# Issuing an activation exchange of 12 transfers a few at a time between weight loads, and placing the splits of an exchanged block ahead of the next transposition

## The chip, the cores and the metric

The kernel runs on one core of one Trainium2 chip. The metric is the device time of one execution in microseconds (us). Of the kernel before there are three timed runs, 964.92, 965.22 and 965.23 us; their median is 965.22 us.

## What is computed

A small encoder: two layers, 256 tokens of width 1024, all in 32-bit floats. Each layer has a feed-forward sub-layer, a token mixer (retention in the first layer, latent attention in the second) beside a cross-attention into 256 memory tokens, and a second feed-forward sub-layer. What the change touches is the feed-forward, of which there are four with inner width 2816:

```python
def swiglu(h, w_gu, w_down):
    g, u = jnp.split(h @ w_gu, 2, axis=-1)
    return (jax.nn.silu(g) * u) @ w_down

for l in range(DEPTH):
    x = x + 0.5 * rms_norm(swiglu(rms_norm(x, ng[0]), ffn_w_gu[l, 0], ffn_w_down[l, 0]), ng[1])
    ...
    x = x + 0.5 * rms_norm(swiglu(rms_norm(x, ng[4]), ffn_w_gu[l, 1], ffn_w_down[l, 1]), ng[5])
```

All weights are read from HBM once per execution, some 180 MB in all.

## The kernel before

**Matmuls.** The 256 tokens are two halves of 128, t = 0 and 1. A float32 product is made of three matmuls (`mm3`, L136 to L138) of operands that are split into a high part of reduced precision and a remainder: high times high, high times low, low times high. A split (`split`, L75 and L76) is a copy on ACT that makes the high part and a subtraction on DVE that makes the low one.

**Weights.** Weights go through tiles of 128 x 1024 floats, 512 KB each. `load_raw` (L79) fills a tile `raw` from HBM, there are five of them; a gate-and-up tile (four per chunk) takes two DMAs of 256 KB (L87), a down tile (two per chunk) one of 512 KB (L89). `split_raw` makes `wh` (ACT) and `wl` (DVE) of it, there are nine of each. So a tile can be loaded at most 14 tiles before the one that TensorE (PE) is working on. All these DMAs are issued by the SP queue, which works in order: a DMA whose semaphores have not come holds back those behind it.

**The feed-forward** (`ffn`) cuts the inner width into 11 chunks c of 256 columns. `gu(t, c)` makes gate and up of a chunk (24 matmuls), `swiglu(t, c)` makes `s` (ACT, L263) and `a` (DVE, L265). `both(c)` multiplies a chunk by its rows of the down weights for both halves (24 matmuls) and needs the chunk's activations with the inner width on the partitions. The order on PE is written out: (0,0), (0,1), (1,0), (1,1) in some order, then (0,2), (1,2), and from c = 3 on gu(0,c), gu(1,c), both(c-3).

**The exchange.** The turning of a chunk is done without PE. `turn(t, c)` (L277 ff.) has DVE transpose blocks of 32 x 32 (STREAM_TRANSPOSE, L282) into a tile `aT` that holds two chunks and both halves. After (1, c) with c odd, 16 pieces of 32 partitions x 256 floats have to change partitions, from `aT` to a tile `ag`, of which there is one: four stay on their partitions and are copied by POOL (L288), twelve are DMAs of 32 KB on the SP queue (L291). This happens at c = 1, 3, 5, 7 and 9 of each of four feed-forwards, 20 times. `take(c)` then splits a chunk of `ag` into `ah` and `al` for both halves, at the `swiglu` named by `landed`: chunk 0 at (0,3), chunk 1 at (1,3), chunk 2 at (0,5) and so on.

```python
if t == 1 and c % 2:
    g = wk.tile([P, 1024], F32, name="ag", tag="ag", bufs=1)
    for i in range(4):
        sl = slice(i * 32, (i + 1) * 32)
        G.tensor_copy(out=g[sl, i * 256:(i + 1) * 256], in_=b[sl, i * 256:(i + 1) * 256])
        for q in range(4):
            if q != i:
                nc.sync.dma_start(out=g[q * 32:(q + 1) * 32, i * 256:(i + 1) * 256],
                                  in_=b[sl, q * 256:(q + 1) * 256])
    pair[c - 1], pair[c] = g, g
```

**What sets the order.** PE's order is that of the program text. On ACT, DVE, POOL and SP a scheduler places instructions by its own estimate of when they are ready; `tc.issue_after(x)` (in `behind` and `behind_weights`) makes it place something behind x.

Of the kernel before, what the change touches and what calls it, by code (L numbers as in the profile page):

```python
# [31 lines left out]
def kernel(ctx, tc, x, mem, positions, norm_gains, ffn_w_gu, ffn_w_down, w_o,  # L32
                        mem_norm, mem_w_kv, ret_w_in, ret_log_decay, ret_head_norm,
                        mla_w_in, mla_q_norm, mla_kv_norm, mla_w_uq, mla_w_ukv, inv_freq, out):
    nc = tc.nc
    V, S, G, T = nc.vector, nc.scalar, nc.gpsimd, nc.tensor
# [17 lines left out]
    def k1(name, n=256, dt=F32):  # L54
        return wk.tile([P, n], dt, name=name, tag="k1", bufs=13)
# [4 lines left out]
    def bank():  # L60
        return ps.tile([P, 512], F32, name="bank", tag="bank")

    def raw_tile():
        return wp.tile([P, 1024], F32, name="raw", tag="raw", bufs=5)
# [12 lines left out]
        return ins  # L77

    def load_raw(src, cols):  # L79
        raw = raw_tile()  # L80
        dst = raw[:, :cols]
        if len(src.shape) == 3:
            dst = dst.rearrange("p (k n) -> p k n", k=src.shape[1])
        if len(src.shape) == 4:
            dst = dst.rearrange("p (k h n) -> p k h n", k=src.shape[1], h=src.shape[2])
            for k in range(src.shape[1]):
                last_load[0] = nc.sync.dma_start(out=dst[:, k], in_=src[:, k]).ins  # L87
        else:
            last_load[0] = nc.sync.dma_start(out=dst, in_=src).ins  # L89
        return raw  # L90

    last_load = [None]

    def behind_weights():

        return tc.issue_after(last_load[0])
# [3 lines left out]
    def behind(*inss):  # L100

        st = ExitStack()
        for i in inss:
            st.enter_context(tc.issue_after(i))
        return st
# [16 lines left out]
    def weights(src, cols):  # L122
        return split_raw(load_raw(src, cols), cols)
# [11 lines left out]
    def mm3(dst, ah, al, bh, bl, start, stop):  # L135
        T.matmul(out=dst, lhsT=ah, rhs=bh, start=start, stop=False)  # L136
        T.matmul(out=dst, lhsT=ah, rhs=bl, start=False, stop=False)  # L137
        T.matmul(out=dst, lhsT=al, rhs=bh, start=False, stop=stop)  # L138
# [65 lines left out]
    def post(t, accs, gain, half, next_gain, hook=None):  # L204
# [19 lines left out]
                hook()  # L224
        return None if next_gain is None else pre(t, next_gain)


    def gu_src(wgu, c, u):
        return (wgu[2 * u * P:(2 * u + 2) * P, :]
                .rearrange("(k p) (h f) -> p k h f", p=P, h=2)[:, :, :, c * FC:(c + 1) * FC])  # L230

    def ffn(l, j, zs, gains, extra=(), first=None):
        wgu, wd = ffn_w_gu[l, j], ffn_w_down[l, j]
        gu_w, d_w, act, at, pair = {}, {}, {}, {}, {}
        accs = [[None, None], [None, None]]
        extra = dict(extra)
        C = NFC - 1

        def load_gu(c):
            gu_w[c] = [weights(gu_src(wgu, c, u), 1024) for u in range(KB // 2)]  # L240

        def load_d(c):
            d_w[c] = [weights(wd[c * FC + b * P:c * FC + (b + 1) * P, :], 1024) for b in range(2)]

        def gu(t, c, part=None):
            z = zs[t]
            if c not in gu_w:
                load_gu(c)
            if part != 1:
                act[t, c] = bank()  # L250
            p = act[t, c]
            for k in range(KB) if part is None else range(part * 4, part * 4 + 4):
                wh, wl = gu_w[c][k // 2]
                n = slice((k % 2) * 512, (k % 2 + 1) * 512)
                m = slice(k * P, (k + 1) * P)
                mm3(p, z.h[:, m], z.l[:, m], wh[:, n], wl[:, n], k == 0, k == KB - 1)
            if part is None:
                swiglu(t, c)

        def swiglu(t, c):  # L260
            p, z = act[t, c], zs[t]
            s = k1("s")
            s_ins = S.activation(out=s, in_=p[:, 0:FC], func=AF.Silu, scale=z.r).ins  # L263
            a = k1("a")
            a_ins = V.scalar_tensor_tensor(out=a, in0=p[:, FC:2 * FC], scalar=z.r, in1=s,  # L265
                                           op0=ALU.mult, op1=ALU.mult).ins
            if (t, c) == (1, NFC - 1) or first and (t, c) == (0, 0):
                ahead[:] = [s_ins, a_ins]
            act[t, c] = a
            if c < C:  # L270
                turn(t, c)
            for k in [k for k in list(pair) if landed(k) == (t, c)]:
                with behind(s_ins, a_ins):
                    take(k)

        def turn(t, c):


            if t == 0 and c % 2 == 0:
                pair[c] = wk.tile([P, 1024], F32, name="aT", tag="aT", bufs=2)  # L280
            b = pair[c - c % 2]
            V.transpose(out=b.rearrange("p (q u t b x) -> p u t q b x", q=4, u=2, t=2, b=2)[:, c % 2, t],  # L282
                        in_=act.pop((t, c)).rearrange("p (b q x) -> p q b x", b=2, q=4))
            if t == 1 and c % 2:
                g = wk.tile([P, 1024], F32, name="ag", tag="ag", bufs=1)
                for i in range(4):
                    sl = slice(i * 32, (i + 1) * 32)
                    G.tensor_copy(out=g[sl, i * 256:(i + 1) * 256], in_=b[sl, i * 256:(i + 1) * 256])  # L288
                    for q in range(4):
                        if q != i:  # L290
                            nc.sync.dma_start(out=g[q * 32:(q + 1) * 32, i * 256:(i + 1) * 256],  # L291
                                              in_=b[sl, q * 256:(q + 1) * 256])
                pair[c - 1], pair[c] = g, g

        def landed(c):

            return (0, min(c + 3, C)) if c % 2 == 0 else (0, C) if c + 2 > C - 1 else (1, c + 2)

        def take(c):
            g = pair.pop(c)  # L300
            ah, al = t2("ah", 512, F32R), t2("al", 512, F32R)
            for t in range(2):
                sl = slice(t * FC, (t + 1) * FC)
                split(g.rearrange("p (i u t b x) -> p u t b i x", i=4, u=2, t=2, b=2)[:, c % 2, t],
                      ah[:, sl].rearrange("p (b i x) -> p b i x", i=4, b=2),
                      al[:, sl].rearrange("p (b i x) -> p b i x", i=4, b=2))
                at[t, c] = ah[:, sl], al[:, sl]

        def tr(t, c):
            a = act.pop((t, c))  # L310
            ah, al = k1("ah", FC, F32R), k1("al", FC, F32R)
            transposed([a[:, 0:P], a[:, P:2 * P]], ah, al)
            at[t, c] = ah, al

        def down(t, c, hs=(0, 1)):
            if c not in d_w:
                load_d(c)
            ah, al = at[t, c]
            for i in hs:
                if c == 0:  # L320
                    accs[t][i] = bank()
                for b in range(2):
                    wh, wl = d_w[c][b]
                    n = slice(i * 512, (i + 1) * 512)
                    m = slice(b * P, (b + 1) * P)
                    mm3(accs[t][i], ah[:, m], al[:, m], wh[:, n], wl[:, n],
                        c == 0 and b == 0, c == NFC - 1 and b == 1)

        def both(c):
            down(0, c)  # L330
            down(1, c)

        if first:
            gu_w[0] = first
            gu(0, 0, 0)
            zs[1].put()
            gu(0, 0, 1)
            swiglu(0, 0)
            gu(1, 0)
            gu(0, 1)  # L340
        else:
            gu(0, 0)
            gu(0, 1, 0)
            zs[1].put()
            gu(0, 1, 1)
            swiglu(0, 1)
            gu(1, 0)
        gu(1, 1)
        gu(0, 2)
        gu(1, 2)  # L350
        for c in range(3, C):
            gu(0, c)
            gu(1, c)
            if c == 4:
                with behind_weights():
                    gain_post, next_gain = gains()
            if c in extra:
                with behind_weights():
                    extra[c]()
            both(c - 3)  # L360
        gu(0, C)
        both(C - 3)
        tr(0, C)
        gu(1, C, 0)
        down(0, C - 2)
        down(0, C - 1)
        down(0, C)
        gu(1, C, 1)
        with in_order():
            z0 = post(0, accs[0], gain_post, True, next_gain, lambda: swiglu(1, C))  # L370
        down(1, C - 2)
        tr(1, C)
        down(1, C - 1)
        down(1, C, (0,))
        if z0:
            z0.put()
        down(1, C, (1,))
        z1 = post(1, accs[1], gain_post, True, next_gain)
        return [z0, z1]
# [764 lines left out]
```

## Time and profile before

| | |
|---|---|
| median of three runs | 965.22 us |
| the profiled execution | 965.5 us, of which its span is 963.7 us and 1.8 us lie around it |
| PE busy | 949.9 us (99%), 4503 matmuls |
| DVE, ACT, POOL busy | 626.2, 516.2, 87.5 us |
| granted TensorE clock | 0.999 of full speed |
| moved by DMA | 189.23 MB, mean 196 GB/s |
| the DMAs | 352 of gate and up at 256 KB, 88 of down at 512 KB, 240 of the exchange at 32 KB |

The profile gives for each engine when it was busy, and for each instruction what it waited for. The four feed-forwards run from about 9 to 196, 324 to 508, 508 to 694 and 774 to 960 us of the span. PE is busy nearly throughout, so what a change is worth shows in the few stretches in which PE starts a matmul later than its predecessor allows, and in how long before its use each tile of weights is ready.

### The profile page before, as it was taken

How to read it: one execution, taken by the hardware profiler on the slowest of the kernel's cores; microseconds unless marked ns; L12 is line 12 of the kernel's file. 1: busy time of each engine (PE TensorE's matmuls, PEld its weight loads, DVE VectorE, ACT ScalarE, POOL GpSimd, SP SyncE). 2: the span in 40 equal slices, each digit the busy share in tenths (PEclk: the TensorE clock that was granted, in tenths of full speed). 3: DMA queues.
4: the chain of work that ended last, by engine and by line, in shares of the span. 5: the costliest groups of instructions: out<-in, count | busy, mean ns of one | idle time of the engine just before them, and what ended most of it. 6: DMA issues, size and time to landing. Idle time of an engine off the chain costs nothing.

```text
span 963.7 us, 13202 instructions
## 1 busy us (share of the span) xinstructions
PE 949.9 (99%) x4503; PEld 789.2 (82%) x4503; DVE 626.2 (65%) x989; ACT 516.2 (54%) x859; POOL 87.5 (9%) x122
## 2 busy tenths in 40 slices
PE   8999999999999999999999999999999999999997
PEld 6887888898878888888887888888897888888886
DVE  6766567586886775655558656655666886566552
ACT  6535456465665654544446444555568864444441
POOL 0110111010000111101101111101010011111010
PEclk9999999999999999999999999999999999999999
DMA  8668677493645556867546676875561746777631
GB/s 276 213 221 274 208 226 249 133 313 103 208 156 162 153 149 234 288 209 211 173 127 204 217 243 223 260 240 165 155 204 32 231 125 198 238 238 225 221 104 44
DMA packets 148679, 189.23 MB, mean 196 GB/s; under 512 B 13314, under 2 KB 130818, under 8 KB 148611
## 3 DMA queue, kind: packets, MB, share of 16 engines
q1 hardware_dynamic: 148608, 188.38, 61.2%
q8 instruction: 35, 0.57, 0.2%
q14 instruction: 34, 0.27, 0.1%
q10 hardware_dynamic: 2, 0.00, 0.0%
HBM read 179.42 MB, written 1.05 MB: 187 GB/s over the span
## 4 chain that ended last, share of the span: by engine, by line
PE 81%; DMA 7%; DVE 4%; ACT 3%; issue 3%; SPq 2%; POOL 0%; DVEq 0%; POOLq 0%; ACTq 0%
PE bank L138 26%; PE bank L136 26%; PE bank L137 26%; DMA raw<-in_ffn_w_gu_dram 4%; PE bank L162 2%; DVE wl L76 2%; ACT wh L75 2%; SPq L291 1%; DMA raw<-in_ret_w_in_dram 1%; DMA raw<-in_ffn_w_down_dram 1%; PE bank L493 1%; SPq L87 1%; ACT e L504 0%; DMA gpre<-in_norm_gains_dram 0%; DVE x L220 0%
## 5 line engine op out<-in xcount | busy, mean ns | idle before, releaser
L76 DVE TENSOR_TENSOR wl<-raw,wh 128x1024 fp32r<-128x1024 f32 (+2 forms) x326 | 388.6, 1209 | 164.6 <-ACT wh L75 158.2
L75 ACT CAST wh<-raw 128x1024 fp32r<-128x1024 f32 (+2 forms) x326 | 334.7, 1042 | 216.5 <-PE bank L138 78.4
L136 PE MATMUL bank<-wh,zh 128*128 128x512 f32 (+2 forms) x944 | 364.5, 386 | 0.6 <-ACT zh L75 0.4
L137 PE MATMUL bank<-wl,zh 128*128 128x512 f32 (+2 forms) x944 | 360.4, 382 | 0.6 <-DVE wl L76 0.6
L138 PE MATMUL bank<-wh,zl 128*128 128x512 f32 (+2 forms) x944 | 360.5, 382 | 0.4 <-DVE zl L76 0.4
L138 PEld LDWEIGHTS bank<-wh,zl 128*128 128x128 f32 x944 | 177.4, 188 | 35.4 <-DVE zl L76 1.4
L136 PEld LDWEIGHTS bank<-wh,zh 128*128 128x128 f32 x944 | 177.6, 188 | 34.8 <-ACT zh L75 0.9
L137 PEld LDWEIGHTS bank<-wl,zh 128*128 128x128 f32 x944 | 177.6, 188 | 34.5 <-DVE wl L76 1.6
L136 PE MATMUL bank<-wh,ah 128*128 128x512 f32 x352 | 138.0, 392 | 0.0
L138 PE MATMUL bank<-wh,al 128*128 128x512 f32 x352 | 137.4, 390 | 0.6 <-DVE al L76 0.6
L137 PE MATMUL bank<-wl,ah 128*128 128x512 f32 x352 | 137.0, 389 | 0.0
L288 POOL COPY ag<-aT 32x256 f32<-32x256 f32 x80 | 55.9, 699 | 481.6 <-DMA raw<-in_ffn_w_gu_dram 290.2
L263 ACT ACTIVATE s<-bank,rstd 128x256 f32<-128x256 f32 x88 | 41.5, 472 | 101.0 <-PE bank L138 100.9
L265 DVE SCALAR_TENSOR_TENSOR a<-bank,rstd,s 128x256 f32<-128x256 f32 x88 | 42.3, 480 | 59.5 <-ACT s L263 59.3
L138 PEld LDWEIGHTS bank<-wh,al 128*128 128x128 f32 x352 | 66.1, 188 | 15.2 <-DVE al L76 1.5
L137 PEld LDWEIGHTS bank<-wl,ah 128*128 128x128 f32 x352 | 66.1, 188 | 13.4
L136 PEld LDWEIGHTS bank<-wh,ah 128*128 128x128 f32 x352 | 66.1, 188 | 13.4 <-ACT ah L75 0.2
L147 ACT ACTIVATE junk<-bank 128x512 bf16<-128x512 f32 x24 | 14.3, 594 | 41.8 <-DVE y L209 29.4
L282 DVE STREAM_TRANSPOSE aT<-a 128x256 f32<-128x256 f32 x80 | 35.4, 443 | 1.5
L75 ACT CAST zh<-bank 128x512 fp32r<-128x512 f32 (+2 forms) x58 | 25.3, 462 | 19.4 <-PE bank L162 12.4
L76 DVE TENSOR_TENSOR zl<-bank,zh 128x512 fp32r<-128x512 f32 (+2 forms) x58 | 28.7, 519 | 6.0 <-ACT zh L75 6.0
L76 DVE TENSOR_TENSOR al<-ag,ah 128x256 fp32r<-128x256 f32 x80 | 31.3, 404 | 1.0 <-ACT ah L75 0.8
(154 smaller groups left out, 519.6 us busy)
## 6 DMA issues: line engine op xcount, KB each, us to landing
raw<-in_ffn_w_gu_dram SPq DMA_DIRECT2D x352, 256.0 KB, 4.7
raw<-in_ffn_w_down_dram SPq DMA_DIRECT2D x88, 512.0 KB, 5.4
raw<-in_ret_w_in_dram SPq DMA_DIRECT2D x48, 256.0 KB, 4.7
raw<-in_w_o_dram SPq DMA_DIRECT2D x16, 512.0 KB, 4.3
ag<-aT SPq DMA_DIRECT2D x240, 32.0 KB, 1.9
raw<-in_mem_w_kv_dram SPq DMA_DIRECT2D x8, 512.0 KB, 5.4
gpost<-in_norm_gains_dram SPq DMA_DIRECT2D x6, 512.0 KB, 6.2
gpre<-in_norm_gains_dram SPq DMA_DIRECT2D x5, 512.0 KB, 7.6
```

The source lines that it names most:

```text
L75: ins = S.copy(out=hi, in_=src).ins
L76: V.tensor_tensor(out=lo, in0=src, in1=hi.bitcast(F32), op=ALU.subtract)
L87: last_load[0] = nc.sync.dma_start(out=dst[:, k], in_=src[:, k]).ins
L136: T.matmul(out=dst, lhsT=ah, rhs=bh, start=start, stop=False)
L137: T.matmul(out=dst, lhsT=ah, rhs=bl, start=False, stop=False)
L138: T.matmul(out=dst, lhsT=al, rhs=bh, start=False, stop=stop)
L147: S.activation(out=junk[:, :h.shape[1]], in_=h, func=AF.Square, scale=scale, accum_out=ss[:, i:i + 1])
L162: T.transpose(out=tp[:s.shape[1], j * P:(j + 1) * P], in_=s, identity=ident)
L263: s_ins = S.activation(out=s, in_=p[:, 0:FC], func=AF.Silu, scale=z.r).ins
L265: a_ins = V.scalar_tensor_tensor(out=a, in0=p[:, FC:2 * FC], scalar=z.r, in1=s, op0=ALU.mult, op1=ALU.mult).ins
L282: V.transpose(out=b.rearrange("p (q u t b x) -> p u t q b x", q=4, u=2, t=2, b=2)[:, c % 2, t], in_=act.pop((t, c)).rearrange("p (b q x) - ...
L288: G.tensor_copy(out=g[sl, i * 256:(i + 1) * 256], in_=b[sl, i * 256:(i + 1) * 256])
```

## The change

The twelve DMAs of an exchange are no longer issued in one run. `exchange` makes the four POOL copies and hands twelve `moves` in groups of n to a list `between`; `load_raw` then lets `skip` tiles pass and issues one group after each further tile, behind that tile's load, and puts the next loads behind the group. At c = 1 skip and n are 4 and 3, at c = 3, 5 and 7 they are 6 and 2, at c = 9 the twelve stay together. In `swiglu` the splits (`take`) are called ahead of `turn`.

```diff
     def load_raw(src, cols):
+        with behind(*moved):
+            return load_now(src, cols)
+
+    def load_now(src, cols):
         raw = raw_tile()
...
             last_load[0] = nc.sync.dma_start(out=dst, in_=src).ins
+        if between:
+            between[0][0] -= 1
+            if between[0][0] < 0:
+                with behind_weights():
+                    moved[:] = [between[0][1].pop(0)()]
+                if not between[0][1]:
+                    between.pop(0)
         return raw
...
+    def exchange(b, g, skip, n):
+        def move(i, q):
+            return nc.sync.dma_start(out=g[q * 32:(q + 1) * 32, i * 256:(i + 1) * 256],
+                                     in_=b[i * 32:(i + 1) * 32, q * 256:(q + 1) * 256]).ins
+        pairs = []
+        for i in range(4):
+            sl = slice(i * 32, (i + 1) * 32)
+            G.tensor_copy(out=g[sl, i * 256:(i + 1) * 256], in_=b[sl, i * 256:(i + 1) * 256])
+            pairs += [(i, q) for q in range(4) if q != i]
+        steps = [lambda p=pairs[k:k + n]: [move(*x) for x in p][-1] for k in range(0, 12, n)]
+        if n == 12:
+            steps[0]()
+        else:
+            between.append([skip, steps])
...
             act[t, c] = a
-            if c < C:
-                turn(t, c)
             for k in [k for k in list(pair) if landed(k) == (t, c)]:
                 with behind(s_ins, a_ins):
                     take(k)
+            if c < C:
+                turn(t, c)
...
             if t == 1 and c % 2:
                 g = wk.tile([P, 1024], F32, name="ag", tag="ag", bufs=1)
...
+                skip, n = (4, 3) if c == 1 else (6, 2) if c < C - 1 else (0, 12)
+                exchange(b, g, skip, n)
                 pair[c - 1], pair[c] = g, g
```

The SP queue around the first exchange (c = 1) of the second feed-forward, before. `raw` is a tile of weights (two gate-and-up DMAs or one down DMA fill it), `ag<-aT` are the transfers of the exchange:

```order
L87 DMA raw<-in_ffn_w_gu_dram 128x2x256 x20
L89 DMA raw<-in_ffn_w_down_dram 128x1024 x2
L87 DMA raw<-in_ffn_w_gu_dram 128x2x256 x4
L291 DMA ag<-aT 32x256 x12
L87 DMA raw<-in_ffn_w_gu_dram 128x2x256 x4
```

and now (12 more gate-and-up DMAs stand ahead of either piece):

```order
L91 DMA raw<-in_ffn_w_gu_dram 128x2x256 x14
L243 DMA ag<-aT 32x256 x3
L91 DMA raw<-in_ffn_w_gu_dram 128x2x256 x2
L243 DMA ag<-aT 32x256 x3
L91 DMA raw<-in_ffn_w_gu_dram 128x2x256 x2
L243 DMA ag<-aT 32x256 x3
L91 DMA raw<-in_ffn_w_gu_dram 128x2x256 x2
L243 DMA ag<-aT 32x256 x3
L93 DMA raw<-in_ffn_w_down_dram 128x1024 x2
L91 DMA raw<-in_ffn_w_gu_dram 128x2x256 x8
```

Before, 20 tiles of weights (16 of chunks 0 to 3, two of down chunk 0, two of chunk 4) stood ahead of the twelve transfers. Now 13 tiles do, and tiles 14, 15 and 16, the last three of chunk 3, each stand behind three transfers more. The queue looks the same at c = 1 of the other three feed-forwards.

The SP queue around the second exchange (c = 3) of the same feed-forward, before (`gpost` and `gpre` are gain vectors of the norms):

```order
L67 DMA gpost<-in_norm_gains_dram 128x1024
L67 DMA gpre<-in_norm_gains_dram 128x1024
L89 DMA raw<-in_ffn_w_down_dram 128x1024 x2
L87 DMA raw<-in_ffn_w_gu_dram 128x2x256 x8
L291 DMA ag<-aT 32x256 x12
```

and now:

```order
L67 DMA gpost<-in_norm_gains_dram 128x1024
L67 DMA gpre<-in_norm_gains_dram 128x1024
L93 DMA raw<-in_ffn_w_down_dram 128x1024
L243 DMA ag<-aT 32x256 x2
L93 DMA raw<-in_ffn_w_down_dram 128x1024
L243 DMA ag<-aT 32x256 x2
L91 DMA raw<-in_ffn_w_gu_dram 128x2x256 x2
L243 DMA ag<-aT 32x256 x2
```

The second tile of down chunk 1 and the four tiles of chunk 5 stood ahead of the exchange and now lie between its pairs of transfers, one tile after each pair; five tiles are moved behind the first transfer. At c = 5 and c = 7 it is the same.

DVE at the same first exchange, before, from `a` of (1,1) on (`wl` is the low part of a tile of weights, `a` the activation, `aT<-a` its transposition, `al` the low part of an exchanged chunk):

```order
L265 SCALAR_TENSOR_TENSOR a<-bank,rstd,s 128x256
L282 STREAM_TRANSPOSE aT<-a 128x4x64
L76 TENSOR_TENSOR wl<-raw,wh 128x1024
L265 SCALAR_TENSOR_TENSOR a<-bank,rstd,s 128x256
L282 STREAM_TRANSPOSE aT<-a 128x4x64
L76 TENSOR_TENSOR wl<-raw,wh 128x1024 x3
L265 SCALAR_TENSOR_TENSOR a<-bank,rstd,s 128x256
L282 STREAM_TRANSPOSE aT<-a 128x4x64
L76 TENSOR_TENSOR wl<-raw,wh 128x1024
L265 SCALAR_TENSOR_TENSOR a<-bank,rstd,s 128x256
L76 TENSOR_TENSOR al<-ag,ah 128x256
L282 STREAM_TRANSPOSE aT<-a 128x4x64
```

and now:

```order
L294 SCALAR_TENSOR_TENSOR a<-bank,rstd,s 128x256
L311 STREAM_TRANSPOSE aT<-a 128x4x64
L294 SCALAR_TENSOR_TENSOR a<-bank,rstd,s 128x256
L311 STREAM_TRANSPOSE aT<-a 128x4x64
L76 TENSOR_TENSOR wl<-raw,wh 128x1024 x2
L294 SCALAR_TENSOR_TENSOR a<-bank,rstd,s 128x256
L311 STREAM_TRANSPOSE aT<-a 128x4x64
L76 TENSOR_TENSOR wl<-raw,wh 128x1024 x2
L294 SCALAR_TENSOR_TENSOR a<-bank,rstd,s 128x256
L76 TENSOR_TENSOR al<-ag,ah 128x256 x2
L311 STREAM_TRANSPOSE aT<-a 128x4x64
```

Ahead of `a` of (1,1) 16 tiles of the block had their `wl` before, now 13; tiles 14 and 15 come behind (0,2), tile 16 behind (1,2). Both `al` of chunk 0 now precede the transposition of (0,3).

## Rows read from the trace of the kernel before

**Rows 1.** The page: busy time, share of the span and instructions of each engine.

```profile
PE 949.9 (99%) x4503; PEld 789.2 (82%) x4503; DVE 626.2 (65%) x989; ACT 516.2 (54%) x859; POOL 87.5 (9%) x122
```

**Rows 2.** Windows: stretch, its length, then busy us (instructions) of each engine, clock, DMA share, GB/s.

```profile
335.00:371.00 36.00, 36.00 (x162) 29.82 (x161) 23.14 (x31) 19.06 (x27) 3.03 (x5) 1.00 0.63 197
376.00:470.00 94.00, 94.00 (x417) 77.82 (x416) 56.98 (x73) 45.62 (x61) 9.17 (x12) 1.00 0.67 215
520.00:556.00 36.00, 36.00 (x160) 29.76 (x160) 22.54 (x30) 18.34 (x26) 2.97 (x5) 1.00 0.60 193
785.00:822.00 37.00, 37.00 (x168) 30.75 (x167) 23.17 (x31) 19.03 (x27) 3.02 (x5) 1.00 0.58 179
```

**Rows 3.** Timeline of PE, start and length in us, at both(0) and both(2), first feed-forward.

```profile
55.84 0.39 PE L137 MATMUL bank<-wl,ah 128*128 128x512 f32 x1
56.26 0.50 PE L138 MATMUL bank<-wh,al 128*128 128x512 f32 x1
...
88.84 0.40 PE L137 MATMUL bank<-wl,ah 128*128 128x512 f32 x1
89.83 0.50 PE L138 MATMUL bank<-wh,al 128*128 128x512 f32 x1 [0.60 <-DVE al L76]
90.17 0.40 PE L136 MATMUL bank<-wh,ah 128*128 128x512 f32 x1
```

**Rows 4.** Chain that ended last, around the first exchange of the first feed-forward: start, us, what.

```profile
35.20 1.06 ACT wh L75
...
36.29 1.23 DVE wl L76
...
37.95 0.46 DVE aT L282
...
38.42 0.60 SPq L291
...
45.39 0.59 SPq L291
...
46.08 0.60 SPq L87
...
46.73 3.17 DMA raw<-in_ffn_w_gu_dram
...
49.97 1.06 ACT wh L75
```

**Rows 5.** Line L291: durations in ns (min/median/max) of its 20 waits on SP.

```profile
L291 SPq EVENT_SEMAPHORE  x20: 17/800/3818, 35.5 to 921.4; - x20
```

**Rows 6.** Timeline of the second feed-forward, where gu(0,2) ends and gu(1,2) begins.

```profile
354.16 0.39 PE L136 MATMUL bank<-wh,zh 128*128 128x512 f32 x1
...
354.36 0.47 ACT L263 ACTIVATE s<-bank,rstd 128x256 f32<-128x256 f32 x1 [2.61 <-PE bank L138]
...
354.87 0.48 DVE L265 SCALAR_TENSOR_TENSOR a<-bank,rstd,s 128x256 f32<-128x256 f32 x1 [1.85 <-ACT s L263]
...
355.39 0.45 DVE L282 STREAM_TRANSPOSE aT<-a 128x256 f32<-128x256 f32 x1
```

**Rows 7.** Timeline of PE, second feed-forward: first matmuls of tile 16, of gu(0,4), of both(1).

```profile
363.68 0.39 PE L136 MATMUL bank<-wh,zh 128*128 128x512 f32 x1
363.91 0.39 PE L137 MATMUL bank<-wl,zh 128*128 128x512 f32 x1
...
375.92 0.39 PE L136 MATMUL bank<-wh,zh 128*128 128x512 f32 x1
...
386.80 0.39 PE L136 MATMUL bank<-wh,ah 128*128 128x512 f32 x1
```

**Rows 8.** Line L87, issue to landing: two DMAs on an idle queue (341.5 to 342.9), then all.

```profile
DMA to landing us min/median/max: 3.2/3.2/3.2
DMA to landing us min/median/max: 2.7/4.7/10.5
```

**Rows 9.** Line L89 (down tiles, 512 KB and less), issue to landing, whole span.

```profile
DMA to landing us min/median/max: 3.2/5.1/10.4
```

More of the change, by code (lines that the diff above doesn't have):

```diff
@@ L89, in load_raw @@
             last_load[0] = nc.sync.dma_start(out=dst, in_=src).ins
+        if between:
[5 more added lines that the diff above has]
+                    between.pop(0)
         return raw
     last_load = [None]
+    between, moved = [], []
     def behind_weights():
@@ L285, in turn @@
                 g = wk.tile([P, 1024], F32, name="ag", tag="ag", bufs=1)
[L286 to L292, printed above, removed]
+                skip, n = (4, 3) if c == 1 else (6, 2) if c < C - 1 else (0, 12)
+                exchange(b, g, skip, n)
                 pair[c - 1], pair[c] = g, g
@@ L299, in take @@
         def take(c):
+            assert not between, between
             g = pair.pop(c)
```

## The prediction

> **What bounds the kernel now.** I read the page's busy times first: PE is busy 949.9 of 963.7 us [rows 1], so no other engine can bound the kernel by itself. A busy PE can still hide waits, since a record of a matmul (0.39 us) overlaps the next; so I then read windows and the starts of single matmuls. In four stretches of the feed-forwards, each around exchanges, PE shows no idle time at all [rows 2]. The starts give the pace: from the first matmul of gu(0,4) at 375.92 to the first of both(1) at 386.80 there are 48 matmuls [rows 7], so 10.88/48 = 0.227 us each; a chunk costs 10.88 us for gate and up and half of that, 5.44 us, for down.
>
> Next I looked for the places where an exchange costs PE something. There are two, both in the first feed-forward. At 56.26 a matmul that needs `al` starts 0.42 us after the one before, 0.19 late, and at 89.83 one starts 0.99 us after, 0.76 late [rows 3]. A restart costs a bit more: the matmul after the late one starts 0.34 us behind it (90.17 against 89.83), 0.11 above the pace [rows 3]. So the two waits cost about 0.3 and 0.9 us, **1.2 us in all**. That is everything the twelve transfers cost PE today, though the burst holds the SP queue for over 7 us each time: the first starts at 38.42, the last at 45.39, the next load of weights is issued at 46.08 [rows 4]. The loads stand far enough ahead of their use to sit through it.
>
> **What the change removes.** No instruction goes and none is added: PE, POOL and the number of DMAs are the same. The twelve transfers cost the same 0.63 us of SP each, (45.39 - 38.42)/11 [rows 4]. What can be won is the 1.2 us above. Both waits were for `al`, held back on DVE behind a `wl` whose tile came late over the burst. With tiles spread between the transfers, and `al` ahead of the transposition, I take both as gone: -1.2 us (ends: 0 and -1.2).
>
> **What the change moves, first exchange (c = 1).** The order shows that 20 tiles stood ahead of the transfers and now 13 do. SP works in order, so after tile 13 it stands before the first transfer until DVE has transposed (1,1), and loads nothing. That it does stand there is seen today, with less at stake: before L291 it waited 0.8 us as a median, 3.8 at most [rows 5]. Tiles 14 to 16 now come after this wait, and PE wants them in gu(0,3). The race, counted from B, the end of gu(1,1), with numbers of the second feed-forward:
>
> - Transposition. At the same point one product later, PE's next starts at 354.16, `s` at 354.36, `a` at 354.87, the transposition ends at 355.39 + 0.45 = 355.84 [rows 6]: B + 1.68. SP issues 0.02 later (37.95 + 0.45 to 38.42) [rows 4]: the first transfer at B + 1.70.
> - Three transfers and a load. Third transfer 1.27 us after the first; next load 0.69 behind it (45.39 to 46.08); second DMA of a tile 0.65 behind its first (46.08 to 46.73) [rows 4]. So the second DMA of tile 14 goes out at B + 4.31. A round (load to transfer, which I take at 0.70 as the nearest, then 1.27, 0.69, 0.65) is 3.31: tile 15 at B + 7.62, tile 16 at B + 10.93.
> - Landing and split. On an idle queue such a DMA lands after 3.2 us [rows 8], and here each has the queue nearly to itself. The cast starts 0.07 after the landing (46.73 + 3.17 = 49.90 to 49.97) and takes 1.06, `wl` follows by 0.03 and takes 1.23 [rows 4]. Tile 16 is ready at B + 10.93 + 3.2 + 0.07 + 1.06 + 0.03 + 1.23 = **B + 16.52**.
> - Wanted. Tile 16's first matmul with `wl` is the twentieth of gu(0,3), which follows 10.88 us of chunk 2: B + 10.88 + 19 x 0.227 = **B + 15.19**. (As a check: with B = 354.16 - 5.44 = 348.72 this is 363.91, where the trace has it [rows 7].)
>
> So PE waits 1.3 us for tile 16, and with the restart 0.11 loses 1.4. Tile 15 is ready at B + 13.2 and wanted at 13.8, tile 14 at 9.9 against 12.5: both in time. The same queue order and PE order stand at c = 1 of all four feed-forwards: 4 x 1.4 = **+5.7 us**.
>
> This hangs on the landing. Its ends are 2.7 us, the least of all [rows 8], and 4.7, the median, which is under load. With 2.7 the loss is 0.9 a time, 3.7 in all. With 4.7 tile 15 is 0.9 late as well, tile 16 by 1.9 more, 3 a time, 12 in all. I take 3.2, because the loads are 3.3 us apart, so that each lands before the next goes out.
>
> The Trainium skill, "DMA: Bandwidth & Descriptors", section "Anatomy of one DMA — SWDGE (gpsimd) path", fits a DMA's time as 2.0 us plus its bytes at 436 GB/s, for another issuing path than this one; my estimate from that is 2.6 us for 256 KB. The row of this case has 3.2. By the page's figure the loss would be 0.8 a time and the forecast 967.4 us instead of the one below.
>
> **Down tiles of chunk 0.** They follow the last three transfers, about B + 13.3 and 13.9. With a landing of 4 to 5 us (3.2 least, 5.1 median [rows 9]), the second is split by about B + 22.9 (DVE has `a` and two `al` in between), and is wanted at B + 10.88 + 10.88 + 1.4 + 0.9 = 24.1. In time by about 1 us: cost nothing, the cover being the stall before it; landing at 6 to 7 us it would cost 1 us a time.
>
> **Exchanges at c = 3, 5, 7.** Five tiles move behind the first transfer, one after each pair, a round of 1.3 + 1.3 = 2.6 us. Counted from the end of gu(1,3), the transposition is later than before by the two `al`, some 0.8 us, so the first pair goes at about 2.5 to 4. The second down tile of chunk 1 follows at once and is wanted only after both(0) and chunk 4, 16.3 us. The last tile of chunk 5 goes out by about 17 us, is ready by 22, and is wanted at 5.44 + 10.88 + 5.44 + 4.1 = 25.8. Slack 4 us or more, the later ones more: nothing. While SP stands before these transfers it loses nothing either, as the raw tiles are full. At c = 9 the burst stays and one tile changes sides, wanted over 20 us later: nothing.
>
> **Splits ahead of the turns.** `al` of 0.4 us comes earlier, the transposition later by as much; neither is waited for by PE at the later exchanges.
>
> **Sum.** 965.5 + 5.7 - 1.2 = 970.0 for the profiled execution. That execution stands 0.3 us above the median of the three runs, so I forecast **969.7 us**, 0.47% slower. What a measurement can tell from no change is taken as 0.2%, 1.9 us: slower begins at 967.1, faster ends at 963.3.
>
> **The rivals.**
> 1. *The weights come in time after all* (not slower). PE loses nothing at c = 1, if SP gets through its first seven issues and the landing 1.4 us sooner than I count; then only the 1.2 us are won: 965.2 - 1.2 = 964.0, no change. It decides at B + 15.19 for tile 16. For it: the sum has seven pieces, and PE in the same rows never waited with this queue. Against: each piece is from a row of the same instructions, and the least landing seen still leaves 0.9. A partial form (0.4 us a time or less) is also within 0.2%. Chance 0.17.
> 2. *It is faster by over 0.2%.* Besides the 1.2 us, starts of later stages would have to gain 0.8 or more. The order shows no change on any engine there, beyond one down tile at each block's end. About 963. Chance 0.03.
> 3. *The loads fall further behind* (slower by more). After the idle stretch, down tiles and those of chunk 4 arrive under load at the 5 to 7 us that many have [rows 9], and both(0) waits too: 1 to 2 us more a time, 974 to 978. For it: 12 transfers, seven tiles and two gains in a row. Against: the 1 us of cover. Chance 0.10.
> 4. *The pieces of the exchange stay together*: excluded by the order, save at c = 9.
>
> **How the numbers follow.** My forecast has 0.70, rival 3 0.10, rival 1 0.17, rival 2 0.03. All of the first two is slower: 0.80; same 0.17; faster 0.03. The forecast's own range is 967.5 (landing 2.7, or by the page's figure) to 972.5 (landing 3.7). The whole range reaches down over part of rival 1, to 965.0, and up to 973.0.
>
> **What would show it.** Right: PE has about 1.3 us of idle before a matmul that reads `wl`, about 15.2 us after gu(1,1) ends, in each feed-forward; SP has four long waits, of 8 to 20 us, ahead of the first transfer at c = 1; the two late `al` of the first feed-forward are gone; nothing is idle at c = 3 to 9. Wrong: no idle there, or a landing far from 3.2 us on lines of the loads between transfers, or new waits at both(0) or in chunk 5.

## The result and the profile after

The change takes 970.32 us (median of four runs, 969.42 to 971.24) against 965.23 us of the kernel before on the same chip: ratio 1.0055, 95% interval 1.0040 to 1.0071, so 0.55% slower. The forecast was 969.7 us in a range of 965 to 973. The profiled execution after is one of 971.24 us with a span of 969.5 us, 5.8 us more than the 963.7 of before.

The page of after has PE at the same number of matmuls and at a busy time 2.5 us longer than in [rows 1] (part of each late start counts as busy, since records overlap: at 365.64 below the starts are 1.26 us apart and the idle time is 0.76):

```profile
PE 952.4 (98%) x4503; PEld 789.8 (81%) x4503; DVE 628.8 (65%) x989; ACT 516.8 (53%) x859; POOL 76.0 (8%) x122
```

PE's instructions by line, after (busy us, mean ns of one, idle time before them and what ended it). L148, L149 and L150 are the three matmuls of `mm3`; before they were L136 to L138:

```profile
L148 PE MATMUL bank<-wh,zh 128*128 128x512 f32 (+2 forms) x944 | 365.4, 387 | 1.4 <-ACT wh L75 1.0 <-ACT zh L75 0.3
L149 PE MATMUL bank<-wl,zh 128*128 128x512 f32 (+2 forms) x944 | 361.7, 383 | 3.0 <-DVE wl L76 3.0
L150 PE MATMUL bank<-wh,al 128*128 128x512 f32 x352 | 137.2, 390 | 0.0
```

The idle time now ends with `wl` and `wh` of gate and up, and `wh,al`, which stood late at 56.26 and 89.83 in [rows 3], has none. Where it lies is seen in the second feed-forward, the one that the prediction computed. First SP around the first exchange, after (start, length of the group in us):

```profile
350.86 1.85 SPq L243 DMA_DIRECT2D ag<-aT  x3
352.81 1.26 SPq L91 DMA_DIRECT2D raw<-in_ffn_w_gu_dram  x2
354.11 1.87 SPq L243 DMA_DIRECT2D ag<-aT  x3
356.08 1.26 SPq L91 DMA_DIRECT2D raw<-in_ffn_w_gu_dram  x2
357.38 1.88 SPq L243 DMA_DIRECT2D ag<-aT  x3
359.36 1.26 SPq L91 DMA_DIRECT2D raw<-in_ffn_w_gu_dram  x2
```

Each group of three transfers is followed by one tile of two DMAs, and a round is 3.27 us (352.81 to 356.08). Tile 16 is the last pair, at 359.36. From issue to landing its two DMAs took, in us:

```profile
DMA to landing us min/median/max: 3.1/3.2/3.2
```

Its cast on ACT follows (timeline; in brackets what ACT waited for):

```profile
363.27 1.05 ACT L75 CAST wh<-raw 128x1024 fp32r<-128x1024 f32 x1 [1.93 <-DMA raw<-in_ffn_w_gu_dram]
```

then its `wl` on DVE:

```profile
364.36 1.23 DVE L76 TENSOR_TENSOR wl<-raw,wh 128x1024 fp32r<-128x1024 f32 x1 [1.25 <-ACT wh L75]
```

and PE behind it:

```profile
363.86 0.39 PE L150 MATMUL bank<-wh,zl 128*128 128x512 f32 x1
364.38 0.50 PE L148 MATMUL bank<-wh,zh 128*128 128x512 f32 x1
365.64 0.50 PE L149 MATMUL bank<-wl,zh 128*128 128x512 f32 x1 [0.76 <-DVE wl L76]
365.98 0.40 PE L150 MATMUL bank<-wh,zl 128*128 128x512 f32 x1
```

The starts are 0.52, 1.26 and 0.34 us apart where the pace is 0.227: 1.44 us lost. In the same way gu(0,3) of the first, third and fourth feed-forward loses 1.52, 2.05 and 1.50 us (0.1 of the third at tile 15, the rest at tile 16). That is 6.5 us in all; the two late `al` of before are gone and save 1.2; the rest of the 5.8 is +0.5 us at starts of stages that the change does not touch. Such starts are not the same from kernel to kernel: one matmul group of the retention (at 267.50 before) starts 0.3 to 1.7 us after the matmul ahead of it over the kernels run here, with the same code there. No matmul at c = 3 to 9 starts late by more than 0.1 us.

The four waits of SP for the transposition at c = 1 (durations in ns, one line for each feed-forward but the first, where SP waited 9.7 us):

```profile
L243 SPq EVENT_SEMAPHORE  x1: 18680/18680/18680, 332.2 to 332.2; - x1
L243 SPq EVENT_SEMAPHORE  x1: 19376/19376/19376, 517.7 to 517.7; - x1
L243 SPq EVENT_SEMAPHORE  x1: 19161/19161/19161, 786.0 to 786.0; - x1
```

Before, the longest of these waits was 3.8 us [rows 5].

### The profile page after: what moved, and what is told of

The parts are those of the page before. It is cut to its first block, busy times and chain, and to the rows that moved or that the text cites. A ratio compares the mean times of both kernels' runs of the same rounds, so it can differ in the third digit from the quotient of the medians.

```text
span 969.5 us, 13111 instructions
## 1 busy us (share of the span) xinstructions
PE 952.4 (98%) x4503; PEld 789.8 (81%) x4503; DVE 628.8 (65%) x989; ACT 516.8 (53%) x859; POOL 76.0 (8%) x122
## 4 chain that ended last, share of the span: by engine, by line
PE 84%; DMA 4%; SPq 4%; DVE 3%; issue 2%; ACT 2%; POOL 0%; DVEq 0%; POOLq 0%; ACTq 0%
PE bank L149 26%; PE bank L150 26%; PE bank L148 26%; PE bank L174 3%; DMA raw<-in_ffn_w_gu_dram 2%; SPq L243 2%; SPq L91 2%; DMA raw<-in_ret_w_in_dram 1%; DVE wl L76 1%; PE bank L519 1%; PE bank L551 1%; ACT wh L75 1%; DMA gpre<-in_norm_gains_dram 0%; DVE x L232 0%; PE bank L771 0%
## 5 line engine op out<-in xcount | busy, mean ns | idle before, releaser
L148 PE MATMUL bank<-wh,zh 128*128 128x512 f32 (+2 forms) x944 | 365.4, 387 | 1.4 <-ACT wh L75 1.0
L149 PE MATMUL bank<-wl,zh 128*128 128x512 f32 (+2 forms) x944 | 361.7, 383 | 3.0 <-DVE wl L76 3.0
L150 PE MATMUL bank<-wh,zl 128*128 128x512 f32 (+2 forms) x944 | 361.2, 383 | 0.4 <-DVE zl L76 0.4
L149 PEld LDWEIGHTS bank<-wl,zh 128*128 128x128 f32 x944 | 177.8, 188 | 38.8 <-DVE wl L76 6.0
L148 PEld LDWEIGHTS bank<-wh,zh 128*128 128x128 f32 x944 | 177.9, 188 | 37.3 <-ACT wh L75 3.1
L150 PEld LDWEIGHTS bank<-wh,zl 128*128 128x128 f32 x944 | 177.8, 188 | 35.1 <-DVE zl L76 1.4
L148 PE MATMUL bank<-wh,ah 128*128 128x512 f32 x352 | 138.0, 392 | 0.0
L150 PE MATMUL bank<-wh,al 128*128 128x512 f32 x352 | 137.2, 390 | 0.0
L149 PE MATMUL bank<-wl,ah 128*128 128x512 f32 x352 | 137.0, 389 | 0.0
L248 POOL COPY ag<-aT 32x256 f32<-32x256 f32 x80 | 44.4, 556 | 511.7 <-DVE aT L311 350.4
L150 PEld LDWEIGHTS bank<-wh,al 128*128 128x128 f32 x352 | 66.1, 188 | 13.8
L149 PEld LDWEIGHTS bank<-wl,ah 128*128 128x128 f32 x352 | 66.1, 188 | 13.4
L148 PEld LDWEIGHTS bank<-wh,ah 128*128 128x128 f32 x352 | 66.1, 188 | 13.4
```

## The experiments

Twelve kernels were run, four beside each other each time. All times are medians; ratios are to the kernel before in the same session (965.33, 964.99 and 964.49 us; for the change 965.23). "B" is the end of gu(1,1), as in the prediction, and is read here as the start of the first matmul of gu(0,2). All kernels are the change with one or two edits. Late starts are summed from the starts of PE's matmuls in each kernel's trace.

| kernel | c = 1 (tiles passed, group) | c = 3, 5, 7 | placing of casts | us | ratio, 95% interval |
|---|---|---|---|---|---|
| the change | 4, 3 | pairs | as is | 970.32 | 1.0055 (1.0040 to 1.0071) |
| splits_only | burst | burst | as is | 964.79 | 0.9998 (0.9989 to 1.0007) |
| late_only | burst | pairs | as is | 970.47 | 1.0055 (1.0043 to 1.0067) |
| first_only | 4, 3 | burst | as is | 979.73 | 1.0150 (1.0137 to 1.0163) |
| first_6_6 | 6, 6 | pairs | as is | 968.60 | 1.0034 (1.0021 to 1.0047) |
| first_4_12 | 4, 12 | pairs | as is | 990.59 | 1.0263 (1.0236 to 1.0290) |
| late_ahead2 | burst | pairs | behind `ah` | 963.65 | 0.9990 (0.9981 to 0.9999) |
| five_ahead2 | 5, 4 | pairs | behind `ah` | 965.14 | 1.0002 (0.9991 to 1.0012) |
| after_ahead2 | 4, 3 | pairs | behind `ah` | 971.54 | 1.0068 (1.0055 to 1.0081) |
| splits_ahead2 | burst | burst | behind `ah` | 977.16 | 1.0129 (1.0114 to 1.0144) |
| late_ahead | burst | pairs | behind `ah`, last chunk too | 994.11 | 1.0302 (1.0282 to 1.0323) |
| six_ahead | 6, 6 | pairs | behind `ah`, last chunk too | 994.13 | 1.0303 (1.0283 to 1.0324) |
| after_ahead | 4, 3 | pairs | behind `ah`, last chunk too | 1001.17 | 1.0374 (1.0355 to 1.0392) |

**The place of the splits alone.**

```diff
-                skip, n = (4, 3) if c == 1 else (6, 2) if c < C - 1 else (0, 12)
+                skip, n = (0, 12)
```

> Splits ahead of the turns, all twelve transfers in one burst at every exchange. Theory: the two late al of the kernel before came from wl queued ahead of them on DVE, whose tiles arrived late over the burst, so the place of the splits alone wins next to nothing: 964.7 to 965.3 us, with one or two late al (0.2 to 0.9 us) still there in the first feed-forward, and no wait at tile 14 to 16 in gu(0,3). Rival: the place of the splits alone removes both late al: 964.0 us.

As expected: no difference that can be measured. On SP and ACT the order is that of the kernel before; only DVE's differs. One late `al` is left, at 56.48, and costs 0.45 us; the second is gone. PE, splits_only:

```profile
56.48 0.50 PE L150 MATMUL bank<-wh,al 128*128 128x512 f32 x1 [0.18 <-DVE al L76]
```

**Only the later exchanges spread.**

```diff
-                skip, n = (4, 3) if c == 1 else (6, 2) if c < C - 1 else (0, 12)
+                skip, n = (0, 12) if c == 1 else (6, 2) if c < C - 1 else (0, 12)
```

> The first exchange (c = 1) is one burst again, c = 3, 5, 7 keep their pairs of transfers between loads, splits ahead of the turns. Theory (the loss is the late loads of tiles 14 to 16 at c = 1): the four waits of 1.4 to 2.0 us in gu(0,3) are gone, 963.8 to 965.3 us, against 970.3 with the change. Rival (spreading the later exchanges costs by itself): 967 us or more, with PE starting late in both(0) or at c = 4 to 9.

The four waits in gu(0,3) are gone, as the theory had it, but its time was missed: the kernel is as slow as the change. PE by line, late_only:

```profile
L148 PE MATMUL bank<-wh,ah 128*128 128x512 f32 x352 | 138.3, 393 | 1.8 <-ACT ah L75 1.8
L150 PE MATMUL bank<-wh,al 128*128 128x512 f32 x352 | 137.6, 391 | 1.8 <-DVE al L76 1.8
```

The idle time has moved to `ah` and `al`. The largest piece, 2.9 us, is at both(2) of the first feed-forward. PE there:

```profile
90.11 0.50 PE L148 MATMUL bank<-wh,ah 128*128 128x512 f32 x1 [1.78 <-ACT ah L75]
...
91.43 0.50 PE L150 MATMUL bank<-wh,al 128*128 128x512 f32 x1 [0.58 <-DVE al L76]
```

and ACT ahead of it:

```profile
85.69 1.05 ACT L75 CAST wh<-raw 128x1024 fp32r<-128x1024 f32 x1 [0.52 <-PE bank L150]
88.34 1.04 ACT L75 CAST wh<-raw 128x1024 fp32r<-128x1024 f32 x1 [1.61 <-PE bank L150]
89.30 0.47 ACT L292 ACTIVATE s<-bank,rstd 128x256 f32<-128x256 f32 x1
89.66 0.70 ACT L75 CAST ah<-ag 128x256 fp32r<-128x256 f32 x2
```

The product that `s` needs was done some 6 us before, but the scheduler had put six casts of weights ahead of `s` and `ah`, and `ah`, which PE wants next, stands behind them. These casts wait for their tiles to land. The profile names PE for the last two, but where an instruction waits for several semaphores that name can be the wrong one, and by the times both start just behind a landing. The tile of the last one was issued here:

```profile
80.92 1.21 SPq L91 DMA_DIRECT2D raw<-in_ffn_w_gu_dram  x2
```

and its two DMAs took

```profile
DMA to landing us min/median/max: 6.7/6.7/6.7
```

The second went out at 81.53 and landed at 88.25, 0.09 us before the cast at 88.34; the tile of the cast at 85.69 landed at 85.59. For their own matmuls the tiles are in time. In the change only five casts stand there in the first feed-forward, and `ah` starts at 84.90.

**Only the first exchange spread.**

```diff
-                skip, n = (4, 3) if c == 1 else (6, 2) if c < C - 1 else (0, 12)
+                skip, n = (4, 3) if c == 1 else (0, 12)
```

> Only the first exchange is spread (three transfers after each of tiles 13 to 16), c = 3, 5, 7 are bursts again, splits ahead of the turns. Theory: the whole loss is here: four waits of 1.4 to 2.0 us in gu(0,3) as with the change, 970 to 971.5 us. Rival (the loss lies with the later exchanges): 967 us or less.

A miss: the waits in gu(0,3) are there (1.49, 1.42, 1.92 and 1.46 us), but 7.7 us more are lost at both(1) of the first three feed-forwards. The scheduler put the burst of c = 3 ahead of both down tiles of chunk 1, where the kernel before has it behind them. SP, first_only:

```profile
61.35 7.54 SPq L243 DMA_DIRECT2D ag<-aT  x12
...
69.56 0.90 SPq L93 DMA_DIRECT2D raw<-in_ffn_w_down_dram  x2
```

and PE, which waits for those tiles:

```profile
74.89 0.51 PE L148 MATMUL bank<-wh,ah 128*128 128x512 f32 x1 [1.59 <-ACT wh L75]
76.15 0.50 PE L149 MATMUL bank<-wl,ah 128*128 128x512 f32 x1 [0.75 <-DVE wl L76]
```

This is the race of c = 1 once more, at another place: twelve transfers behind a late transposition, and behind them the tile that PE wants next. The pairs of the change let the first down tile go ahead and the second after two transfers.

**Two groups of six.**

```diff
-                skip, n = (4, 3) if c == 1 else (6, 2) if c < C - 1 else (0, 12)
+                skip, n = (6, 6) if c == 1 else (6, 2) if c < C - 1 else (0, 12)
```

> At c = 1 two groups of six, after tiles 15 and 16, so that only tile 16 stands behind transfers (six); c = 3, 5, 7 in pairs as in the change. Theory (race of tile 16): first transfer at B + 1.7, six transfers 3.2 us, second DMA of tile 16 at B + 6.2, ready at B + 11.8 against B + 15.2 wanted: no wait, 963.8 to 965.0 us, although the transfers are still spread. Rival (SP's stand before the first transfer costs by itself, or spreading does): 967 us or more.

No wait in gu(0,3), as expected; the second DMA of tile 16 goes out at B + 6.2. The time was missed: as in late_only, PE waits for `ah` and `al`, at both(0), both(2) and both(4) of the first feed-forward, and in the third and fourth, 5.2 us in all. PE by line, first_6_6:

```profile
L150 PE MATMUL bank<-wh,al 128*128 128x512 f32 x352 | 137.8, 392 | 2.6 <-DVE al L76 2.6
```

So two causes were mixed, and the next edit was made to take them apart: the casts of all later tiles are placed behind the `ah` of each even chunk.

```diff
             for k in [k for k in list(pair) if landed(k) == (t, c)]:
                 with behind(s_ins, a_ins):
-                    take(k)
+                    ins = take(k)
+                if t == 0:
+                    ahead[:] = ins
```

`take` returns the two ACT instructions, and `ahead` is what `split_raw` already stands behind. It was put on late_only, on first_6_6 and on the change.

> As the run with c = 1 in one burst and c = 3, 5, 7 in pairs (970.5 us), but the casts of all later tiles are placed behind the ah split of each even chunk on ACT. Theory (the waits for ah and al in both(2) and later there came from the place on ACT and DVE: casts of late tiles ahead of s and ah): those waits, 5 us in all, go away, 964 to 965.5 us. Rival (the tiles themselves come too late when the transfers are spread): PE waits for wh or wl in their place, 968 us or more.

> As the run with two groups of six at c = 1 (968.6 us), with the same placing of casts behind ah. Theory: neither the waits in gu(0,3) nor those for al, 964 to 965.5 us. Rival: waits for weights in both(c), 967 us or more.

> The change itself with the same placing of casts behind ah. Theory (two separate mechanisms, of which the change as it is shows only the race of tiles 14 to 16): the four waits in gu(0,3) stay at 1.4 to 2.0 us each, 969 to 971 us. Rival (one lag of the loads that shows at one place or another): 966 us or less, or waits at other places.

All three failed by their times: 994.11, 994.13 and 1001.17 us. In each feed-forward 6.6 to 8.9 us are lost at one place (part of it in matmuls 0.43 us apart), after gu(0,10), where the edit put the down tiles of chunk 7, wanted at once, behind the splits of chunks 8 and 9. PE, late_ahead:

```profile
170.24 0.55 PE L148 MATMUL bank<-wh,ah 128*128 128x512 f32 x1 [4.04 <-ACT wh L75]
```

Up to that place, though, late_ahead had no wait at an exchange and stood 1.45 us ahead of the kernel before. So the four last runs have the same edit, ended before the last chunk (`if t == 0 and c < C`).

> As the first run with c = 1 in one burst, c = 3, 5, 7 in pairs and casts of later tiles behind ah, but that placing ends before the last chunk, where it had put the down tiles of chunk 7 behind the splits of chunks 8 and 9 and cost 27 us. Theory: up to that place PE stood 1.4 us ahead of the kernel before, and nothing else waits, so 963 to 965 us. Rival (weights late over the spread exchanges, now hidden by the longer waits): 967 us or more.

As expected. PE by line, late_ahead2:

```profile
L150 PE MATMUL bank<-wh,al 128*128 128x512 f32 x352 | 137.1, 390 | 0.0
```

and ACT at the place that was shown of late_only:

```profile
83.24 0.47 ACT L292 ACTIVATE s<-bank,rstd 128x256 f32<-128x256 f32 x1 [6.58 <-PE bank L150]
83.61 0.70 ACT L75 CAST ah<-ag 128x256 fp32r<-128x256 f32 x2
84.21 4.85 ACT L75 CAST wh<-raw 128x1024 fp32r<-128x1024 f32 x5
```

`ah` is cast 6 us earlier and the five casts follow it without a gap. The difference between late_only and this kernel (970.47 and 963.65 us; spans of 967.8 and 962.2) is the place of the casts: the transfers are spread alike in both, and on SP only three or four down tiles near the end of each feed-forward are issued later. It is the fastest kernel of the study, 0.1% below the kernel before; that is half of what was called measurable here, though its interval just leaves out 1.

> The change with the same placing of casts, ended before the last chunk. Theory: the four waits in gu(0,3) stay, 1.5 to 2.2 us each as in the run that had it to the end, 6.5 to 7 us in all, no wait at both(c): 969 to 971.5 us. Rival (the place of the casts makes the waits at c = 1 too): 966 us or less.

As expected, with a time just above the upper end: the waits in gu(0,3) are 1.45, 1.58, 1.90 and 1.47 us, 6.4 in all, and nothing waits at both(c):

```profile
L149 PE MATMUL bank<-wl,zh 128*128 128x512 f32 (+2 forms) x944 | 361.5, 383 | 3.1 <-DVE wl L76 3.0
```

> c = 1 in three groups of four, after tiles 14, 15 and 16 (the change: four groups of three, after 13 to 16), c = 3, 5, 7 in pairs, casts behind ah as above. Theory: the first transfer at B + 1.7, tile 16 behind eight transfers and tile 15, second DMA at B + 8.9, ready at B + 14.5 against B + 15.2 wanted: in time by 0.7, no wait in gu(0,3), 963 to 965.5 us. Rival (spreading costs as such, so nearly as much as four groups of three): 968 us or more.

As expected. Its edit differs from that of after_ahead2 by where the groups stand at c = 1 and by nothing else, SP's order of weights and transfers differs nowhere but there, and it is 6.4 us faster. The start of gu(0,2) on PE and tile 16 on SP in the second feed-forward, five_ahead2:

```profile
347.08 0.39 PE L148 MATMUL bank<-wh,zh 128*128 128x512 f32 x1
...
355.30 1.26 SPq L91 DMA_DIRECT2D raw<-in_ffn_w_gu_dram  x2
```

and DVE at tile 16, the tile of the last pair:

```profile
360.32 1.23 DVE L76 TENSOR_TENSOR wl<-raw,wh 128x1024 fp32r<-128x1024 f32 x1 [2.51 <-ACT wh L75]
```

B is 347.08, and `wl` is ready at 361.55: B + 14.47, where 14.5 was expected.

> All exchanges in one burst, splits ahead of the turns, casts behind ah as above. Theory (the 1.2 us of late al are a matter of place on ACT and DVE, not of the burst): both late al of the first feed-forward gone, 963.3 to 964.8 us, as good as with c = 3, 5, 7 spread. Rival (spreading the later exchanges is what brings al in time): 965 us or more, late al still there.

A miss: both late `al` are gone, but with all exchanges in bursts the new placing again brings the burst of c = 3 ahead of the down tiles of chunk 1 (8.56 us on SP, the down tiles behind it), and in the first and third feed-forward that of c = 5 ahead of one of chunk 3. PE by line, splits_ahead2:

```profile
L148 PE MATMUL bank<-wh,ah 128*128 128x512 f32 x352 | 139.7, 397 | 3.1 <-ACT wh L75 3.1
L149 PE MATMUL bank<-wl,ah 128*128 128x512 f32 x352 | 139.1, 395 | 4.8 <-DVE wl L76 4.6
```

So a burst is harmless only where the tiles wanted next are ahead of it in the queue, as they are in the kernel before.

**All twelve transfers after tile 13.**

```diff
-        if n == 12:
+        if n == 12 and not skip:
             steps[0]()
...
-                skip, n = (4, 3) if c == 1 else (6, 2) if c < C - 1 else (0, 12)
+                skip, n = (4, 12) if c == 1 else (6, 2) if c < C - 1 else (0, 12)
```

> At c = 1 all twelve transfers stand in one burst after tile 13, so nothing is spread there, but tiles 14 to 16 wait for all twelve; c = 3, 5, 7 in pairs. Theory (the price is the position behind the transposition, not the spreading): twelve transfers and the loads put the second DMA of tile 14 at B + 10.0, ready at B + 15.6 against B + 12.5 wanted: 3.2 us and the restart at tile 14 in each gu(0,3), 13 us in all, 976 to 979 us. Rival (going to and fro between transfers and loads is what costs): less than the change, 968 us or less.

The rival fell: with nothing spread at c = 1 the loss is larger, so the position is what costs. The position was computed well: `wl` of tile 14 is ready at 369.18, which is B + 15.6, as expected (gu(0,2) starts at 353.61; the burst at 355.34). The time was not: 990.6 instead of 976 to 979 us, since each feed-forward lost 5.8 to 8.3 us and not 3.3. PE, first_4_12:

```profile
367.97 0.62 PE L148 MATMUL bank<-wh,zh 128*128 128x512 f32 x1 [1.96 <-ACT wh L75]
369.23 0.79 PE L149 MATMUL bank<-wl,zh 128*128 128x512 f32 x1 [0.64 <-DVE wl L76]
369.82 0.63 PE L150 MATMUL bank<-wh,zl 128*128 128x512 f32 x1
370.25 0.63 PE L148 MATMUL bank<-wh,zh 128*128 128x512 f32 x1
```

The two waits make 3.2 us, as computed. But after them the matmuls start 0.43 us apart instead of 0.227, up to 374.67, with one more wait for `wl` (tile 15, at 372.36) among them.

## Why the prediction was right, point by point

- **The race of tile 16.** In the second feed-forward B is the start of this matmul:

```profile
349.12 0.39 PE L148 MATMUL bank<-wh,zh 128*128 128x512 f32 x1
```

The first transfer is at B + 1.74 against the 1.70 of the text; the second DMA of tile 16 goes out at 360.01, B + 10.89 against 10.93; landing 3.2 against 3.2; `wl` ready at 365.59, B + 16.47 against 16.52; lost 1.44 us against 1.4. In all four it is 6.5 against 5.7. The difference is mostly the third feed-forward. There tile 15's pair took 1.86 us to issue where it is 1.26 elsewhere, so tile 16 came 0.6 later:

```profile
542.34 1.86 SPq L91 DMA_DIRECT2D raw<-in_ffn_w_gu_dram  x2
```

Such an issue was in no case of the prediction; the slow landing that it did allow for (4.7) did not come to tile 16. The profiled execution lies 1.2 us above the 970.0 of the sum: 0.8 of it is this race and 0.5 the starts of other stages, which the sum left out. The figure of the Trainium skill that was weighed there ("DMA: Bandwidth & Descriptors", section "Anatomy of one DMA — SWDGE (gpsimd) path", by which 256 KB were estimated at 2.6 us) does not fit this queue: 3.1 to 3.2 us were measured for tile 16, so the row was the better basis.
- **That the loss belongs to the position in the queue** is shown by five_ahead2 against after_ahead2 (6.4 us for one table entry) and by first_4_12, where `wl` of the first late tile comes at the computed moment too. By the count, tile 16 is 3.4 us ahead of its use with (6, 6) and 0.7 us with (5, 4), and no more than 0.2 us was lost, once; with (4, 3) it is 1.3 us behind, and that is the wait of the change.
- **The 1.2 us of the late `al`.** Their size was right, and both are gone. The reason was only half right. The text gave it to spread transfers and to splits ahead of the transposition; splits_only shows that the second takes away one of them, and late_only, which spreads the transfers of the late exchanges, has worse ones. What decides is which casts of weights stand ahead of `s` and `ah` on ACT, and when their tiles land.
- **"Exchanges at c = 3, 5, 7: nothing", and `al` "neither is waited for by PE at the later exchanges".** This holds in the change, but the working behind it was incomplete. It compared when tiles are ready with when they are wanted, and never looked at ACT, where the change moves `ah` too. late_only and first_6_6 have the same pairs at c = 3, 5 and 7 and lose 5 us there. Whether the change is spared by its order of casts or by the 1.5 us that PE loses at c = 1 was not separated by a run. In its trace `al` of the first half is ready 1.7 us or more ahead of its matmul at every exchange; the least is at both(0) of the first feed-forward, just after 1.52 us were lost, so without that loss less than 0.2 us would be left there by this count. That nothing waited there was in part luck. late_ahead2 shows that the order alone can be enough.
- **Rival 1** was priced wrongly by this: with the weights in time it said 964.0 us, and the kernels that spread the later exchanges and have the weights in time give 968.6 and 970.5 us, as long as ACT's order is left to the scheduler. With that order mended they give 963.65 and 965.14.
- **Down tiles of chunk 0** were in time, and rival 3 did not come: nothing waits at both(0). The four waits of SP are there, with 9.7 to 19.4 us. PE's idle time stands before matmuls with `wl`, which start about 1.3 us later than they were wanted (0.13 and 0.76 us of it show as idle in the second feed-forward). Two figures of the text are off by its own working, without weight for the forecast: after a round of 3.31 us the down tiles go out at about B + 13.6 and 14.2 and not 13.3 and 13.9 (13.5 and 14.1 were measured), and a landing of 3.7 us gives 971.8 us and not 972.5.

## What to carry to other kernels

When DMAs that wait for a result share an in-order queue with loads, count from the moment of the result, not from the average lead of the loads: what stands behind the first waiting DMA starts its way through the queue only then, and the next tile wanted has to win that race by itself. Moving DMAs also moves what a scheduler does with the engines behind them, so read the order on every engine between the load and the consumer: here the same transfers cost 5 us or nothing by the place of a few casts on ACT that waited for tiles not wanted yet. An experiment that "takes one part alone" needs the same look, since in four of the kernels here the scheduler moved something else too.

## What the runs showed of the hardware that was not expected

TensorE's granted clock can fall after a wait inside a busy stretch, and here the fall cost nearly as much as the idle time (about 2 us beside 2.6). The windows of first_4_12 (stretch and length, then busy us and instructions of PE, PEld, DVE, ACT and POOL, granted clock, DMA share, GB/s):

```profile
356.00:366.00 10.00, 10.00 (x45) 7.95 (x43) 0.93 (x2) 0.48 (x1) 0.96 (x3) 1.00 0.29 81
366.00:370.00 4.00, 1.40 (x4) 0.86 (x4) 1.62 (x2) 1.42 (x2) 0.00 (x0) 0.78 1.00 272
370.00:374.00 4.00, 3.80 (x10) 2.50 (x9) 2.59 (x3) 2.58 (x3) 0.00 (x0) 0.50 0.99 367
376.00:380.00 4.00, 4.00 (x19) 3.34 (x18) 4.00 (x7) 3.18 (x6) 0.00 (x0) 1.00 0.92 280
```

PE was busy at the full 2.4 GHz, waited twice (2.0 and 0.6 us idle), and then ran at 0.50, the 1.2 GHz level, before it came back to 1.00. At that level some ten matmuls cost 0.2 us more each, about 2 of the 3 us that the expectation missed in this feed-forward; most of the rest is the wait for tile 15. In the change itself, where PE sat idle for about 1 us, the granted clock stays at 1.00 through the wait (window 364 to 366). The length of the waits alone does not tell: in first_only PE was idle for 1.6 and then 0.8 us around 75 and stayed at 1.00, and in splits_ahead2 it was idle for 0.9 and then 1.4 us around 110 and fell to 0.50, which is part of that kernel's time too. The windows of the two, first_only ahead:

```profile
74.00:78.00 4.00, 2.00 (x6) 1.16 (x7) 3.03 (x4) 3.33 (x5) 0.00 (x0) 1.00 1.05 365
111.00:114.00 3.00, 3.00 (x7) 2.42 (x8) 3.00 (x5) 2.15 (x3) 0.00 (x0) 0.50 0.72 218
```

What sets the boundary was not studied.
